# A hybrid SSD and dilated-attention block on one Trainium2 core: the value projection with weights stationary and tokens moving

## The chip, the core and the metric

The kernel runs on one core of a Trainium2 chip. A core has a matrix engine (TensorE, in the profile PE for matmuls and PEld for loads of the stationary operand), three engines for elementwise work (VectorE or DVE, ScalarE or ACT, GpSimd or POOL) and a queue that issues DMAs (SyncE or SP). The engines run side by side and meet at semaphores; each takes its instructions in order. TensorE writes to PSUM, and VectorE and ScalarE bring results from there to SBUF.

The metric is the device time in microseconds of one execution of the whole block. The profile is of one such execution.

## The reference, cut to what matters

One layer, 1024 tokens, width 1024, all in float32. A normalised input `h` is multiplied by one wide matrix `w_in`, whose columns are split over a state-space branch (SSD), an attention branch and two gates:

```python
h = rmsnorm(x, norm_mix[l])
proj = h @ w_in[l]
z, xBC, dt_raw, qkv, gate_logits = jnp.split(proj, offs[1:], axis=-1)
...
qkv = qkv.astype(jnp.float32).reshape(b, S, 3, ATT_N_HEADS, ATT_HEAD_DIM)
q = rope(qkv[:, :, 0], pos)
k = rope(qkv[:, :, 1], pos)
v = qkv[:, :, 2]
y_att = dilated_attention_branch(q, k, v).reshape(b, S, ATT_OUT_DIM).astype(x.dtype) @ w_att_out[l]
```

There are 12 heads of 128 features in three groups of four. The groups differ in their dilation: a head of the second group lets token t see tokens t, t-4, t-8 and so on, so its tokens are sorted into residue classes, and attention runs in blocks of 128 tokens of one class. After attention the three groups are mixed per token, then come the gates, an output projection, and a SwiGLU feed-forward.

## The kernel before

**Dense units.** All projections are cut into units that TensorE works through one after the other. Each float32 operand is split into a rounded part (hi) and a remainder (lo), and each product takes three matmuls (`mm3`, L336): hi with hi, hi with lo, lo with hi. The normalised input lies in SBUF as `hhi` and `hlo`, with features on the partitions and the 1024 tokens in natural order along the free dimension. A unit writes into one of two wide PSUM pieces (`wide`, 1024 float32 columns, two banks); `wide_now` (L325) takes one, and the task that brings the result out frees it.

There are two kinds of units. `unit_a` (L462) makes 128 output features for all 1024 tokens: the weights are the stationary operand, 512 tokens move, 2 x 8 x 3 = 48 matmuls; the result has features on the partitions. `unit_b` (L474) makes 256 output features for 512 tokens: 128 tokens of `hhi` or `hlo` are stationary, 256 columns of weights move, 2 x 4 x 4 x 3 = 96 matmuls; the result has tokens on the partitions. Which tokens are stationary is said by a function `sel`. For the value projection it is `sel_dil` (L1073): with stride r, the 128 tokens of block b are r elements apart in `hhi`:

```python
res.append(t[:, k, :].rearrange("p (l r) -> p r l", r=4)[:, b // 2, (b % 2) * P:(b % 2 + 1) * P])
```

`STRIDE = (1, 4, 8)` (L41) gives r for the three groups. So the values leave PSUM as rows of tokens in block order, which is how the product of probabilities and values wants them.

**Weights.** `plan` (L344) makes a list of loads in the order of use; `w_dma` fetches the next one over SP (512 KB each), and `w_split` (L354) makes hi on ScalarE (a cast) and lo on VectorE. `pump` keeps at most three loads ahead.

**Order.** The instruction streams are written by a planner, `Pace` (L174). It holds an own time for TensorE and the other engines from a table of costs (`cost`, L188; it knows nothing of strides). Everything but the dense units is a generator: it yields the tiles it waits for, and is continued when the planner believes that they are due. It is looked at only in `tick` (L383), which a unit calls after every second k-tile, that is after six matmuls in `unit_a` and after twelve in `unit_b`. So background work enters TensorE's queue at these places, and if a tile is late against the plan, TensorE waits with all that stands behind.

**Attention.** Two halves (`sp`), three groups each, two heads per half and group. For such a pair the units were: key and query of the first head, two `unit_b` for the values of both heads (L1125), key and query of the second head. `rope_task` (L837) rotates keys and queries and writes them sorted by residue class; it needs three free slabs for a key and two for a query (`slabs`, SBUF pieces of 1024 columns, L312). `v_task` (L867) copies values out of PSUM on ScalarE, 512 columns at a time. `head_bg` (L880) does the attention of one head in the background: scores, exponentials, transposes of the probabilities into one of four PSUM banks (`bank`, L315), product with the values. The heads run one after the other (`att_bg`, L1050); `stats_out` and `combine` (L994) mix the groups and store the result in DRAM (`att_d`). Behind the attention units follow 16 gate units, the first 12 of which run while the last of this is still under way (L1284). The last group of the state-space branch runs beside the first pair.

Of the kernel before, what the change touches and what calls it, by code (L numbers as in the profile page):

```python
# [18 lines left out]
DRAM = bass.MemoryType.DRAM  # L19

P = 128
S = 1024
# [15 lines left out]
QKV0 = DT0 + NH  # L38
GATE0 = QKV0 + 3 * 12 * P

STRIDE = (1, 4, 8)  # L41
# [31 lines left out]


class Buf:
    """A tile in a slot that goes back to its owner on free()."""

    def __init__(self, owner, slot, shape, dt):
        n = math.prod(shape[1:])
# [10 lines left out]
    def free(self):  # L90
        self.owner.pieces.append(self.slot)
        self.slot = None


class Slot:
    """A place in a pool; every use of it is a tile of its own type."""

    def __init__(self, pool, name, width):
        self.pool, self.name, self.width, self.n = pool, name, width, 0
# [4 lines left out]


class Store:
    """Slots of equal size, handed out in the order in which they came back."""

    def __init__(self, pieces, pace=None):
        self.pieces = deque(pieces)  # L110
# [34 lines left out]


class Engine:
    """Passes calls on to an engine and notes when their results are due."""

    def __init__(self, real, pace, kind):  # L150
        self.real, self.pace, self.kind = real, pace, kind
# [20 lines left out]


class Pace:  # L174
    """Emission order: dense tensor work in small pieces, and other tasks as soon as their inputs are due."""

    def __init__(self):
        self.t = 0.0
# [117 lines left out]
def hybrid_block(ctx, tc, x, norm_mix, w_in, b_gate, conv_w, conv_b, dt_bias, a_log, d_skip, ssm_norm,  # L296
                 w_ssm_out, w_att_out, w_mix_out, norm_ffn, w_ffn_gate, w_ffn_up, w_ffn_down, norm_final,
                 consts, rope, out):
    pace = Pace()
    nc = Core(tc.nc, pace)  # L300
    x, out = x[0], out[0]
    w_in, w_ssm_out, w_att_out, w_mix_out = w_in[0], w_ssm_out[0], w_att_out[0], w_mix_out[0]
# [9 lines left out]
    slabs = Store([Slot(cpool, f"slab{i}", 1024) for i in range(N_SLAB - 6)])  # L312
    halves = Store([Slot(hfp, f"half{i}", 512) for i in range(12)])
    wide = Store([Slot(pp, f"wide{i}", 1024) for i in range(2)])
    bank = Store([Slot(pp, f"bank{i}", 512) for i in range(4)], pace)  # L315
# [9 lines left out]
    def wide_now():  # L325
        while not wide.pieces:
            pace.idle()
        return wide.get([P, 1024])
# [4 lines left out]
    def tp(o, i, ident):  # L333
        nc.tensor.transpose(o, i, ident)
# [3 lines left out]
        mm(o, lh, rl, False, False)  # L338
        mm(o, ll, rh, False, last)

    # ---------------------------------------------------------------- weight stream
    loads, wstate = [], {"dma": 0, "split": 0, "use": 0}

    def plan(src, nk):  # L344
        loads.append({"src": src, "shape": [P, nk, src.shape[-1]]})
        return len(loads) - 1
# [24 lines left out]
    def w_get(i):  # L371
        while wstate["split"] <= i:
            while wstate["dma"] <= i:
                w_dma()
            w_split()
        wstate["use"] = i
        return loads[i]["w"]
# [5 lines left out]
    def tick():  # L383
        pump()
        pace.due()

    def cols_of(w, k0, nk, c0, nc_):
        return w[k0 * P:(k0 + nk) * P, c0:c0 + nc_].rearrange("(k p) c -> p k c", p=P)
# [20 lines left out]
    def small(tag, w):  # L409
        return cpool.tile([P, w], F32, tag=f"{tag}{w}", name=f"{tag}{w}_{nid()}", bufs=4)  # L410

    # ---------------------------------------------------------------- scratch in DRAM
    acs_d = dr.tile([NCH * NH, P], F32, name="acs_d")
    ea_d = dr.tile([NCH * NH, P], F32, name="ea_d")
    yt_d = [[dr.tile([P, 4, 256], F32, name=f"yt_d{g}_{q}") for q in range(4)] for g in range(NG)]
# [2 lines left out]
    att_d = [dr.tile([P, S], F32, name=f"att_d{i}") for i in range(4)]  # L418
    x2_d = dr.tile([S, D], F32, name="x2_d")

    # ---------------------------------------------------------------- constants and small parameters
    ident = cpool.tile([P, P], F32, name="ident")
    nc.sync.dma_start(ident, consts[:, C_ID:C_ID + P])
    par = cpool.tile([P, 152], F32, name="par")
# [8 lines left out]
    dcol = cpool.tile([P, 16], F32, name="dcol")  # L433
    ysum = cpool.tile([P, NG, NCH], F32, name="ysum")

    # ---------------------------------------------------------------- generic dense units
    hhi = hp.tile([P, KD, S], F32R, tag="hhi", name="hhi")
    hlo = hp.tile([P, KD, S], F32R, tag="hlo", name="hlo")

# [3 lines left out]
    def plan_b(w, col):  # L443
        return [plan(cols_of(w, kh * 4, 4, col, 256), 4) for kh in range(2)]

    class Pair:
        """Two banks in place of a wide piece."""

        def __init__(self):
            while len(bank.pieces) < 2:  # L450
# [23 lines left out]
    def unit_b(lids, sel, last):  # L474
        ps = wide_now()
        for kh in range(2):
            hi, lo = w_get(lids[kh])
            for j in range(4):
                sl = slice(j * 256, j * 256 + 256)
                for kk in range(4):  # L480
                    k = kh * 4 + kk
                    lh, ll = sel(k, j)
                    mm3(ps.v[:, sl], lh, ll, hi[:, kk, :], lo[:, kk, :], k == 0 and j % 2 == 0, k == KD - 1 and j % 2 == 1)
                tick()
            if last:
                w_done(lids[kh])
        return ps

    # ================================================================ state-space branch
    eslabs = Store([slabs.pieces.popleft() for _ in range(2)])  # L490
    grp = [dict() for _ in range(NG)]
    seen = set()
# [56 lines left out]
        grp[g]["CT"] = u  # L549

    class Quarters:
        """Four slabs of a group, each with a quarter of the tokens of its four feature tiles."""

        def __init__(self, g, name, f):
            self.g, self.name, self.f = g, name, f
# [272 lines left out]
        ea.free()  # L828
        pace.fire("dt")

    # ================================================================ attention branch
    rp = {}
    maskA = cst[:, C_MA - P:C_MA - P + 512]
    maskB = cst[:, C_MB - P:C_MB]
    att = {}
# [28 lines left out]
            rp[1].free()  # L864
        pace.fire(f"qk{which}_{head}")

    def v_task(h0, th, ps):  # L867
        if th == 0:
            yield from slabs.room(2)
            for i in range(2):  # L870
                att["v", h0 + i] = slabs.get([P, 8, P])
        v = ps.v.rearrange("p (j c) -> p j c", j=4)
        yield [ps]
        for i in range(2):
            nc.scalar.copy(att["v", h0 + i].v[:, th * 4:(th + 1) * 4, :], v[:, :, i * P:(i + 1) * P])
        ps.free()
        if th == 1:
            pace.fire(f"v{h0}")

    def head_bg(sp, gi, i):  # L880
        head = gi * 4 + sp * 2 + i
        yield f"qk0_{head}"
        yield f"qk1_{head}"
        yield f"v{gi * 4 + sp * 2}"
        yield [att[0, head], att[1, head], att["v", head]]
        q, k, v = att[0, head].v, att[1, head].v, att["v", head].v
        r = STRIDE[gi]
# [7 lines left out]
        for b0 in range(0, 8, step):  # L895
            yield from bank.room()
            yield from halves.room()
            ps, scb = bank.get([P, 512]), halves.get([P, 512])
            sc = scb.v
            segs = []  # L900
            for bi in range(step):
                b = b0 + bi
# [11 lines left out]
            four = lambda a: a.rearrange("p (a b) -> p a b", a=4)  # L914
# [20 lines left out]
            pt, pT = bank.get([P, 512]), halves.get([P, 512])  # L935
# [130 lines left out]
        t.free()  # L1066
        pace.fire(f"gate{i}")

    # ================================================================ dense programme of the input projection
    def sel_nat(th):  # L1070
        return lambda k, j: (hhi[:, k, (th * 4 + j) * P:(th * 4 + j + 1) * P], hlo[:, k, (th * 4 + j) * P:(th * 4 + j + 1) * P])

    def sel_dil(r, th):  # L1073
        def sel(k, j):
            b = th * 4 + j
            res = []
            for t in (hhi, hlo):
                if r == 1:
                    res.append(t[:, k, b * P:(b + 1) * P])
                elif r == 4:  # L1080
                    res.append(t[:, k, :].rearrange("p (l r) -> p r l", r=4)[:, b // 2, (b % 2) * P:(b % 2 + 1) * P])
                else:
                    res.append(t[:, k, :].rearrange("p (l r) -> p r l", r=8)[:, b, :])
            return res
        return sel

    units = []

    def add_a(col, task):
        lids = plan_a(col)  # L1090

        def run(ps=None):
            ps = unit_a(lids, ps)
            pace.spawn(task(ps), 0.0, -1)
        units.append(run)

    def add_b(col, sels, tasks):
        lids = plan_b(w_in, col)
        for th in range(2):
            def run(th=th):  # L1100
                ps = unit_b(lids, sels[th], th == 1)
                pace.spawn(tasks[th](ps), 0.0, -1)
            units.append(run)

    def add_z(g):
        for f in range(4):
# [10 lines left out]
    first = [plan_a(XBC0 + DI)[0], plan_a(XBC0 + DI + 512)[0]]  # L1117
# [4 lines left out]
    def add_qk(which, gi, head):  # L1122
        add_a(QKV0 + (which * 12 + head) * P, lambda ps: rope_task(which, head, STRIDE[gi], ps))

    for sp in range(2):  # L1125
        for gi in range(3):
            h0 = gi * 4 + sp * 2
            add_qk(1, gi, h0)
            add_qk(0, gi, h0)
            add_b(QKV0 + (24 + h0) * P, [sel_dil(STRIDE[gi], 0), sel_dil(STRIDE[gi], 1)],  # L1130
                  [lambda ps, th=th, h0=h0: v_task(h0, th, ps) for th in range(2)])
            add_qk(1, gi, h0 + 1)
            add_qk(0, gi, h0 + 1)
    n_before_gates = len(units)
    for i in range(16):
        add_a(GATE0 + i * P, lambda ps, i=i: gate_task(i, ps))

    # ================================================================ normalised input, transposed; first units on its quarters
    xts = [slabs.get([P, D]) for i in range(NCH)]
    nm, ptmp = slabs.get([P, D]), slabs.get([P, 2, P])  # L1140
    jks = [slabs.get([P, D]) for i in range(2)]
# [153 lines left out]
    halves = Store([Slot(hfp, f"last{i}", 512) for i in range(2)])  # L1295
    slabs.pieces.extend(eslabs.pieces)

    # ================================================================ gated merge, output projection, second norm
    mplans = []
    for th in range(2):  # L1300
        for o in range(KD):
# [158 lines left out]
    for th in range(2):  # L1460
# [10 lines left out]
        for cb in range(4):  # L1471
            def sel(k, j):
                pace.until(f"mx{th}{k}")
                return (h2["hi"][:, 1, k, j * P:(j + 1) * P], h2["lo"][:, 1, k, j * P:(j + 1) * P])

            ps = unit_b(mplans[th * 12 + 8 + cb], sel, True)
            pace.spawn(mo_task(th, cb, ps), 0.3, -1)

    # ================================================================ feed-forward
    act = {}  # L1480

    def ffn_task(f, th, ps):
# [50 lines left out]
    order = [(th, k) for th in range(2) for k in range(KF)]  # L1533
# [56 lines left out]
    for th in range(2):  # L1590
        outs = {}
        tiles = (0, 1, 2, 3) if th else (2, 3, 0, 1)
# [73 lines left out]
```

## Time and profile before

| | |
|---|---|
| median of three runs | 2450.73 us (2450.6 to 2452.07) |
| the profiled execution, from its first to its last instruction | 2448.2 us |
| instructions | 29021 |
| attention's units, first key unit to first gate unit | about 587 to 1185 us |
| mean granted TensorE clock | 0.993 |
| DMA, mean over the span | 90 GB/s |

The page gives no time for the profiled execution other than its span; the median of the runs is 2.5 us above it.

How to read it: a row of the page or of a view names the engine, the operation, the tile written and the tiles read (`out<-in`, with the running number of each tile), the shapes as partitions x elements, and a count or times. Nearly all rows have the line L157, that of the helper that passes calls on to the engines, so tiles tell instructions apart: `wide__33_7663` is one use of a wide PSUM piece, so one unit. A matmul's duration runs from its start to its modelled end, and matmuls overlap; how fast they follow one another is seen in their starts.

### The profile page before, as it was taken

The page shows a single profiled execution, that of the slowest core. Times are in us where ns is not written, and L with a number is a line of the kernel's source. Part 1 is how long each engine was busy: PE and PEld are TensorE (multiplying, and loading weights), DVE is VectorE, ACT ScalarE, POOL GpSimd, SP SyncE. Part 2 cuts the span into 40 slices and gives each one's busy share as a digit, 9 for nine tenths or more (in the row PEclk, how much of TensorE's full clock was granted, in tenths as well). Part 3 has the DMA queues.
Part 4 walks back from the last instruction along what each step waited for, and adds up shares of the span by engine and source line. Part 5 has one row for each costly group of instructions (what it writes and reads, how often), then busy time and mean ns, then how long its engine had stood idle before and what let it go on. Part 6 is the DMA issues. An engine that isn't in the chain of part 4 may idle for free. (4 is left out here: it accounts for less than half of the span.)

```text
span 2448.2 us, 29021 instructions
## 1 busy us (share of the span) xinstructions
PE 2395.4 (98%) x11952; PEld 2021.1 (83%) x11952; DVE 1067.9 (44%) x1542; ACT 734.3 (30%) x1293; POOL 315.8 (13%) x196
## 2 busy tenths in 40 slices
PE   6999999999999999999999998999999999999998
PEld 6887878878889988989888887889888888888786
DVE  6557485765642334332442246534312222233544
ACT  3335253443532233231323224323211111123332
POOL 3005041241520112010040003000000000000101
PEclk8999999999999999999999999999999999999999
DMA  3124242332411013011274456454111111123242
GB/s 122 51 74 122 69 121 73 104 102 88 121 44 35 18 44 112 18 44 27 65 239 127 137 158 196 137 166 127 44 42 45 52 52 44 44 98 117 95 155 78
DMA packets 255016, 220.72 MB, mean 90 GB/s; under 512 B 17132, under 2 KB 226980, under 8 KB 254884
## 3 DMA queue, kind: packets, MB, share of 16 engines
q1 hardware_dynamic: 254884, 218.87, 29.4%
q8 instruction: 94, 1.54, 0.3%
q14 instruction: 38, 0.31, 0.0%
HBM read 191.18 MB, written 27.66 MB: 89 GB/s over the span
## 5 line engine op out<-in xcount | busy, mean ns | idle before, releaser
L157 POOL TENSOR_TENSOR xr<-xr,nfin 128x512 f32<-128x512 f32 x16 | 20.3, 1299 | 915.7 <-ACT jk L157 915.7
L157 POOL TENSOR_TENSOR slab__13_10497<-slab__13_10497,last__3_10482 128x1024 f32<-128x1024 f32 x1 | 2.4, 2409 | 178.9 <-DMA slab__13_10497<-yt_d 178.9
L157 POOL TENSOR_TENSOR half__1_1316<-slab__2_1111,dcol 128x512 f32<-128x512 f32 x1 | 1.0, 1044 | 130.0 <-DVE slab__2_1111 L157 130.0
L157 ACT ACTIVATE jk<-xr 128x512 f32<-128x512 f32 x16 | 10.0, 625 | 24.3 <-DVE xr L157 24.3
L157 PE MATMUL wide__50_10579<-slab__44_10622,h2hi 128*128 128x256 f32 x16 | 5.4, 337 | 6.8 <-DVE slab__44_10622 L157 6.8
L157 ACT ACTIVATE xr<-xr,or 128x512 f32<-128x512 f32 x8 | 5.8, 724 | 17.6 <-DVE or L157 17.6
L157 DVE TENSOR_TENSOR slab__21_6711<-slab__23_6648,slab__20_6710 128x1024 fp32r<-128x1024 f32 x1 | 1.2, 1226 | 21.9 <-ACT slab__20_6710 L157 21.9
L157 DVE TENSOR_TENSOR slab__30_8576<-slab__33_8513,slab__27_8575 128x1024 fp32r<-128x1024 f32 x1 | 1.2, 1225 | 21.9 <-ACT slab__27_8575 L157 21.9
L157 DVE SCALAR_TENSOR_TENSOR ot<-or,ov 128x1 f32<-128x1 f32 x24 | 10.2, 427 | 0.6
L157 POOL TENSOR_TENSOR slab__9_8030<-slab__9_8030,slab__6_4726 128x1024 f32<-128x1024 f32 x1 | 2.4, 2395 | 61.2 <-ACT slab__9_8030 L157 61.2
L157 POOL TENSOR_TENSOR slab__6_6165<-slab__6_6165,slab__6_4726 128x1024 f32<-128x1024 f32 x1 | 2.4, 2398 | 61.2 <-ACT slab__6_6165 L157 61.2
L157 POOL TENSOR_TENSOR slab__7_6789<-slab__7_6789,slab__6_4726 128x1024 f32<-128x1024 f32 x1 | 2.4, 2412 | 60.5 <-ACT slab__7_6789 L157 60.5
L157 POOL TENSOR_TENSOR slab__10_8654<-slab__10_8654,slab__6_4726 128x1024 f32<-128x1024 f32 x1 | 2.4, 2412 | 60.5 <-ACT slab__10_8654 L157 60.5
L157 PE MATMUL wide__1_156<-hhi,slab__1_223 128*128 128x256 f32 x32 | 10.1, 316 | 0.0
L157 PE MATMUL wide__1_156<-hlo,slab__1_223 128*128 128x256 f32 x32 | 9.8, 307 | 0.2 <-DVE hlo L157 0.2
L157 PEld LDWEIGHTS wide__50_10579<-slab__44_10622,h2hi 128*128 128x128 f32 x16 | 3.8, 238 | 7.0 <-DVE slab__44_10622 L157 7.0
L157 PE MATMUL wide__1_157<-hhi,slab__1_274 128*128 128x256 f32 x32 | 9.0, 282 | 0.6 <-DVE slab__1_274 L157 0.6
L157 PE MATMUL wide__1_156<-hhi,slab__1_224 128*128 128x256 f32 x32 | 9.6, 299 | 0.0
L157 DVE TENSOR_TENSOR rt<-rs 128x2 f32<-128x2 f32 (+2 forms) x30 | 9.0, 301 | 1.0
L157 PE MATMUL wide__1_157<-hhi,slab__1_273 128*128 128x256 f32 x32 | 9.3, 291 | 0.0
L157 PE MATMUL wide__1_157<-hlo,slab__1_273 128*128 128x256 f32 x32 | 9.0, 281 | 0.0
L157 PE MATMUL bank__1_158<-ident 128*128 128x128 f32 x36 | 6.3, 357 | 2.6 <-DMA ident<-in_consts 2.6
(6145 smaller groups left out, 8396.5 us busy)
## 6 DMA issues: line engine op xcount, KB each, us to landing
xr<-x_d SPq DMA_DIRECT2D x8, 512.0 KB, 7.3
out<-xr SPq DMA_DIRECT2D x16, 256.0 KB, 2.2
slab__1_123<-in_x SPq DMA_DIRECT2D x1, 512.0 KB
slab__1_124<-in_x SPq DMA_DIRECT2D x1, 512.0 KB
slab__1_131<-in_norm_mix SPq DMA_DIRECT2D x1, 512.0 KB
slab__1_138<-in_w_in SPq DMA_DIRECT2D x1, 512.0 KB, 7.9
slab__1_125<-in_x SPq DMA_DIRECT2D x1, 512.0 KB
slab__1_126<-in_x SPq DMA_DIRECT2D x1, 512.0 KB
```

The source lines that it names most:

```text
L157: r = call(*args, **kw)
```

## The change

The values become a `unit_a` for each head, like keys and queries: the weights of 128 features are stationary, 512 tokens in natural order move. The result has features on the partitions. `v_task` copies it out of PSUM on ScalarE and reads it sorted by residue class (r elements apart) while writing it in one piece into a slab `t`. Then eight transposes on TensorE, four to a PSUM bank, turn it into rows of tokens, and two copies on ScalarE bring these to the slab `V`. The order of the units of a head is key, query, value; a head waits for its own values instead of the pair's. Loads of the value weights have 8 k-tiles of 128 columns instead of 4 k-tiles of 256.

```diff
-    def v_task(h0, th, ps):
-        if th == 0:
-            yield from slabs.room(2)
-            for i in range(2):
-                att["v", h0 + i] = slabs.get([P, 8, P])
-        v = ps.v.rearrange("p (j c) -> p j c", j=4)
+    def v_task(head, r, ps):
+        yield from slabs.room(2)
+        t, V = slabs.get([P, S]), slabs.get([P, 8, P])
         yield [ps]
-        for i in range(2):
-            nc.scalar.copy(att["v", h0 + i].v[:, th * 4:(th + 1) * 4, :], v[:, :, i * P:(i + 1) * P])
+        nc.scalar.copy(t.v.rearrange("p (r l) -> p r l", r=r), ps.v.rearrange("p (l r) -> p r l", r=r))
         ps.free()
-        if th == 1:
-            pace.fire(f"v{h0}")
+        yield [t]
+        for q in range(2):
+            yield from bank.room()
+            pt = bank.get([P, 4, P])
+            for j in range(4):
+                b = q * 4 + j
+                tp(pt.v[:, j, :], t.v[:, b * P:(b + 1) * P], ident)
+            yield [pt]
+            nc.scalar.copy(V.v[:, q * 4:(q + 1) * 4, :], pt.v)
+            pt.free()
+        t.free()
+        att["v", head] = V
+        pace.fire(f"v{head}")
 
     def head_bg(sp, gi, i):
         head = gi * 4 + sp * 2 + i
         yield f"qk0_{head}"
         yield f"qk1_{head}"
-        yield f"v{gi * 4 + sp * 2}"
+        yield f"v{head}"
...
     for sp in range(2):
         for gi in range(3):
-            h0 = gi * 4 + sp * 2
-            add_qk(1, gi, h0)
-            add_qk(0, gi, h0)
-            add_b(QKV0 + (24 + h0) * P, [sel_dil(STRIDE[gi], 0), sel_dil(STRIDE[gi], 1)],
-                  [lambda ps, th=th, h0=h0: v_task(h0, th, ps) for th in range(2)])
-            add_qk(1, gi, h0 + 1)
-            add_qk(0, gi, h0 + 1)
+            for head in (gi * 4 + sp * 2, gi * 4 + sp * 2 + 1):
+                add_qk(1, gi, head)
+                add_qk(0, gi, head)
+                add_a(QKV0 + (24 + head) * P, lambda ps, head=head, gi=gi: v_task(head, STRIDE[gi], ps))
```

The functions `sel_nat`, `sel_dil` and `add_b` go; some comments and docstrings go too, which changes no instruction.

More of the change, by code (lines that the diff above doesn't have):

```diff
@@ L1067, in gate_task @@
         pace.fire(f"gate{i}")
[L1070 to L1085, printed above, removed]
     units = []
@@ L1095, in add_a @@
         units.append(run)
[L1097 to L1103, printed above, removed]
     def add_z(g):
```

## The prediction

> **What bounds the kernel now.** I read the page's busy times and its 40 slices first, to see which engine has no slack.
>
> ```profile
> PE 2395.4 (98%) x11952; PEld 2021.1 (83%) x11952; DVE 1067.9 (44%) x1542; ACT 734.3 (30%) x1293; POOL 315.8 (13%) x196
> ...
> PE   6999999999999999999999998999999999999998
> ...
> PEclk8999999999999999999999999999999999999999
> ```
>
> TensorE is busy in 98% of the span, ScalarE in 30%, VectorE in 44%, at a full granted clock after the first slice. "Busy" says that a matmul is in flight, not that it goes at its best rate. So the next view is the windows over the attention part of the input projection; its columns are the window, its length, busy time and count of instructions of PE, PEld, DVE, ACT and POOL, clock, DMA share and GB/s.
>
> ```profile
> 927.00:949.00 22.00, 22.00 (x196) 22.00 (x196) 7.30 (x21) 3.98 (x6) 7.17 (x3) 1.00 0.33 94
> 1005.00:1054.00 49.00, 49.00 (x228) 48.84 (x226) 10.30 (x11) 8.15 (x16) 2.38 (x1) 1.00 0.05 12
> 1054.00:1110.00 56.00, 55.84 (x279) 46.65 (x279) 25.91 (x31) 20.23 (x43) 7.19 (x3) 1.00 0.17 48
> 1110.00:1159.00 49.00, 49.00 (x217) 48.98 (x216) 7.92 (x11) 6.57 (x15) 2.39 (x1) 1.00 0.11 22
> ```
>
> The first row is the value projection of a stride-1 pair of heads, the second that of a stride-4 pair, the fourth that of a stride-8 pair; the third is four key and query units. The two strided V stages take 49 us for hardly more matmuls than the stride-1 stage does in 22. Their PEld column is full: weights are being loaded all the time, while DVE and ACT have next to nothing to do. This stage is bound by TensorE's weight loads, and no other engine waits behind it.
>
> To price one matmul I take the tile view, whose rows give duration (min/median/max) and the first and last start. Each row's 16 instructions stand at every third place, so 45 starts lie between the two times.
>
> ```profile
> L157 PEld LDWEIGHTS wide__31_7171<-slab__21_6893,hhi x16: 187/188/188, 938.1 to 943.2; 128*128 128x128 f32 x16
> L157 PE MATMUL wide__31_7171<-slab__21_6893,hhi x16: 276/276/276, 938.2 to 943.3; 128*128 128x256 f32 x16
> ...
> L157 PEld LDWEIGHTS wide__34_7802<-slab__27_7591,hhi x16: 332/332/333, 1043.2 to 1053.8; 128*128 128x128 f32 x16
> L157 PE MATMUL wide__34_7802<-slab__27_7591,hhi x16: 402/402/402, 1043.3 to 1053.9; 128*128 128x256 f32 x16
> ...
> L157 PEld LDWEIGHTS wide__37_8436<-slab__29_8223,hhi x16: 337/337/337, 1147.2 to 1158.0; 128*128 128x128 f32 x16
> L157 PE MATMUL wide__37_8436<-slab__29_8223,hhi x16: 403/403/403, 1147.4 to 1158.2; 128*128 128x256 f32 x16
> ...
> L157 PE MATMUL wide__40_8979<-hhi,slab__63_8825 x16: 388/388/388, 1223.9 to 1234.2; 128*128 128x512 f32 x16
> ```
>
> Start to start, a 256-column matmul takes 5.1/45 = 0.113 us at stride 1, 10.6/45 = 0.236 us at stride 4 and 10.8/45 = 0.240 us at stride 8. A 512-column one of a gate unit (the last row; key and query units run the same code) takes 10.3/45 = 0.229 us. Only the stationary operand differs between the first three: 128 token columns next to each other, or 4 or 8 elements apart. The strided weight load lasts 332 to 337 ns instead of 188 and can't hide behind 256 moving columns.
>
> **The change part by part.**
>
> *V matmuls.* Each of the six pairs has two units of 96 matmuls: 4 units, 384 matmuls, of each stride. Removed: 384 x 0.113 = 43.4, 384 x 0.236 = 90.6 and 384 x 0.240 = 92.2, together 226.2 us. Added: 12 units of 48 matmuls over 512 columns, weights stationary and tokens in natural order: 576 x 0.229 = 131.9 us. Difference **-94.3 us**, all on the path, since PE has no idle time in these windows.
>
> *Transposes.* 12 heads x 8, in 24 groups of four. The timeline of TensorE shows such a group of the attention background between matmuls of a unit:
>
> ```profile
> 1002.35 0.39 PE L157 MATMUL wide__33_7569<-hhi,slab__23_7435 128*128 128x512 f32 x1
> 1002.58 0.60 PE L157 MATMUL bank__68_7646<-ident,half__19_7621 128*128 128x128 f32 x4
> 1002.93 0.48 PE L157 MATMUL wide__33_7569<-hhi,slab__23_7434 128*128 128x512 f32 x1
> 1003.25 0.39 PE L157 MATMUL wide__33_7569<-hlo,slab__23_7434 128*128 128x512 f32 x1
> ```
>
> From the group's start to the second wide matmul behind it are 0.67 us; less one wide matmul (0.23) the group costs 0.44 us, its disturbance of the stream included. 24 x 0.44 = **+10.6 us**. The Trainium skill, page "TensorE: Matmul & The Clock Gate", section "Part 4: PE-mode transpose", speaks against the change here: it gives about 275 ns for one 128x128 transpose inside a kernel, and by that, as an estimate, the 96 would cost 26.4 us. The row above gives 0.11 us each, so the row decides; the page's price is kept below as a rival.
>
> *Waiting for the copy out of PSUM.* This is the new wait. The first four transposes of a head stand in PE's queue at the first tick behind the V unit's end, that is behind six matmuls of the next unit: 6 x 0.229 = 1.37 us. They wait for ScalarE's copy of all 1024 tokens. Behind them in PE's in-order queue stands the whole next unit, so a late copy stops TensorE. These rows bound it:
>
> ```profile
> L157 PE MATMUL wide__34_7802<-slab__23_7526,hhi x16: 396/402/485, 1030.6 to 1042.6; 128*128 128x256 f32 x16
> ...
> 1030.81 0.58 ACT L157 COPY slab__9_7815<-wide__33_7663 128x512 f32<-128x512 f32 x1 [2.96 <-PE wide__33_7663 L157]
> ...
> L157 ACT ACTIVATE slab__11_9055<-wide__40_8979,par x1: 1127/1127/1127, 1235.1 to 1235.1; 128x1024 f32<-128x1024 f32 x1
> ...
> 1037.77 0.69 DVE L157 COPY slab__10_7390<-bank__69_7765 128x512 f32<-128x512 f32 x1 [11.05 <-PE bank__69_7765 L157]
> ...
> 1135.91 1.08 DVE L157 COPY slab__11_8029<-bank__78_8378 128x512 f32<-128x512 f32 x1 [8.43 <-PE bank__78_8378 L157]
> ...
> 1170.95 1.19 DVE L157 COPY slab__9_8211<-bank__79_8626 128x512 f32<-128x512 f32 x1 [3.33 <-PE bank__79_8626 L157]
> ```
>
> ScalarE starts 0.2 us after a unit's end (the next unit begins at 1030.6, the copy at 1030.81). A contiguous pass over 1024 PSUM columns takes 1.13 us, so it ends 1.33 us behind the unit, just ahead of the transposes: no wait. Whether reading PSUM 4 or 8 elements apart is slower on ScalarE no row shows. The only strided copies are VectorE's, which write strided: 1.08 and 1.19 us against 0.69, a factor of 1.57 and 1.72. By these the copy takes 1.77 and 1.94 us, and PE would wait 0.60 and 0.77 us for each of the 4 heads of either stride: 4 x 0.60 + 4 x 0.77 = 5.5 us. Below, nothing excludes that it is as fast as the contiguous one: 0. Above, doubling both factors' excess (2.13 and 2.45 times the contiguous pass) gives 4 x 1.23 + 4 x 1.60 = 11.3 us. I take **+5.5 us**, from the rows nearest in having a stride. The Trainium skill, page "Advanced Engine Details and Errata", section "Memory Cachelines", says that consecutive PSUM elements should come in adjacent pairs for best throughput; it gives no time. By it the sum would keep these 5.5 us, and without it would drop them; no row of this run shows which.
>
> *ScalarE and the pieces.* Out go 24 copies of 512 columns, in come 12 of 1024 and 24 of 512: about 12 x 1.13 = 13.6 us more on ScalarE (1.8 times that if strided reads are slow), which has 70% idle. The wide PSUM piece goes back 1.3 to 2.2 us behind its unit and is wanted one unit, 11 us, later. If that cover went, each head would cost the excess of the copy over 11 us.
>
> *Loads.* Two loads of 512 KB per pair stay two; their rows in DRAM shrink from 1 KB to 512 B, which key and query loads have already, and these run at a DMA share of 0.17 without PE idling (third windows row, 55.84 of 56). SP issues them in the same queue, one per 11 us where there were two per 49. Cost: 0, covered by three loads ahead.
>
> *Background.* The second head's V unit moves behind its key and query units, and each head can start when its own V is ready. Heads run one after the other. In the third windows row a unit with background takes 56/4 = 14 us, so three units offer a head some 41 us. I see no new bound. The tail after the last head is the combine, whose last store is at 1254.4; the gate units that cover it run to 1322.8:
>
> ```profile
> L157 SPq DMA_DIRECT2D att_d<-slab__10_7390 x1: 320/320/320, 1254.4 to 1254.4; - x1
> ...
> 1185.40:1322.80 137.40, 136.69 (x618) 112.49 (x617) 57.14 (x60) 42.56 (x62) 32.99 (x13) 1.00 0.55 169
> ```
>
> So up to 68 us of delay of that tail relative to the gates are free. What follows the gates keeps its distances.
>
> **Sum.** 2448.2 - 94.3 + 10.6 + 5.5 = 2370.0 us for the span. The page gives no other time for this execution; the median of the three runs, 2450.73, is 2.5 us above it, which I leave as it is: **2372.5 us**, 3.2% less.
>
> **The rivals.**
>
> *The transposes wait longer* (0.11).
>
> ```profile
> L157 ACT COPY slab__9_8030<-wide__34_7925 64x1024 f32<-64x1024 f32 x2 | 2.0, 1010 | 2.2 <-PE wide__34_7925 L157 2.2
> ...
> L157 ACT CAST slab__24_7932<-slab__59_7886 128x1024 fp32r<-128x1024 f32 x1 | 1.0, 1048 | 10.7 <-DMA slab__59_7886<-in_w_in 10.7
> ```
>
> PE's queue is in order, and a copy that finds a weight cast (1.05 us) or the two copies of a rope unit (2.0 us) ahead of it comes that much later, at every head: 12 x 1 to 12 x 2 = 12 to 24 us more: 2385 to 2397. For it: the emission order rests on planned times. Against: the V copies of before started 0.2 us after their unit.
>
> *The price of a transpose is higher* (0.03). A group placed directly behind a unit could lose more of the stream than the one shown; at 0.275 us each they add 15.8 us: 2388. The page on TensorE named above has this figure; the rows contradict it.
>
> *The gain is not handed on* (0.03). Attention's chain, or the gate stage behind it, sets the end. With the attention part shortened but its background not, the combine would have to slip by more than 68 us; half of the gain lost, 42 us, gives 2415. Against: 41 us offered per head, and PE never idles there now.
>
> *Slower than before: slabs* (0.03). A V task now takes two slabs at once for each head while it holds its wide piece. If they come free only when a background head ends, the unit after next can't start. The saving is 94.3 - 10.6 = 83.7 us, or 7.0 us per head; one further unit (11 us) still runs, so the change loses from a wait of 18 us per head on. At a whole head's 41 us it is 12 x 30 = 360 us, near 2730. Against: a key rope takes three slabs at a time now, and PE has 0.16 us idle in 1054 to 1110. With head h0 starting before K1 and Q1 arrive, fewer tiles are alive, not more.
>
> *The change doesn't do what it says* (0.01). If 256 moving columns and not the stride made the slow rate, stride 1 would show it; it has 0.113.
>
> **How the numbers follow.** The forecast has 0.79; within it the copy may cost 0 to 11.3 us, 2367 to 2378.3, and the stage's other small waits some us either way (beside the first pair runs the last group of the state-space branch, where PE is idle for 1.9 of 102.8 us):
>
> ```profile
> 587.40:690.20 102.80, 100.90 (x681) 85.31 (x680) 67.68 (x107) 52.19 (x108) 46.68 (x33) 1.00 0.39 111
> ```
>
> That makes 2361 to 2384. Its reach with part of the first two rivals holds 8 in 10: 2361 to 2388. Faster by over 0.2% (5 us, about what a measurement here can tell): forecast, first, second and third rival, 0.96. Slower: the slab rival, 0.03. Within 0.2%: 0.01.
>
> **What would show it.** V units as 48 matmuls at 0.229 us for every stride, no PEld row of 330 ns in the attention part; 96 transposes in groups of 0.44 us; the strided copy's duration on ScalarE, near 1.1 (then about 2367) or 1.8 to 1.9 us; PE idle in front of the first group of a head. The forecast is wrong if PE waits more than 2 us at the transposes, or if wide pieces come back late.

## The result, and the profile after

The changed kernel takes 2365.89 us (median of four runs, 2364.59 to 2366.54) against 2451.16 us before (2450.6 to 2452.07): ratio 0.9653, 95% interval 0.964 to 0.9667. That is 85.3 us less; the prediction had said 78.2 us less (2372.5 us). The profiled execution has a span of 2364.8 us against 2448.2, 83.4 us less.

The page's busy times and slices after:

```profile
PE 2310.4 (98%) x11472; PEld 1911.0 (81%) x11472; DVE 1070.8 (45%) x1542; ACT 747.4 (32%) x1305; POOL 316.4 (13%) x196
...
PE   6999999999999999999999989999999999999997
...
PEclk8999999999999999999999989999999999999999
```

TensorE is still the bound at 98%. PE has 480 matmuls fewer: 1152 of 256 columns went, 576 of 512 columns and 96 transposes came. ScalarE has 13 us more work, as counted, and no matmul of the attention stage waits for it. To see where the time went, the windows view is taken over the same three stretches of both kernels: the attention units, the 16 gate units, and all that follows. Before:

```profile
587.40:1185.40 598.00, 595.08 (x3144) 534.62 (x3143) 243.57 (x313) 191.69 (x399) 104.09 (x57) 1.00 0.20 54
...
1185.40:1366.70 181.30, 180.59 (x809) 148.51 (x808) 62.05 (x64) 50.76 (x70) 32.99 (x13) 1.00 0.50 156
1366.70:2448.20 1081.50, 1054.20 (x5009) 876.15 (x5007) 394.37 (x572) 259.33 (x393) 40.70 (x24) 0.99 0.31 98
```

After:

```profile
588.00:1099.80 511.80, 509.94 (x2656) 424.12 (x2655) 250.22 (x315) 203.82 (x410) 107.29 (x58) 1.00 0.24 63
...
1099.80:1281.00 181.20, 181.20 (x817) 149.37 (x816) 57.69 (x62) 51.17 (x71) 30.78 (x12) 1.00 0.51 156
1281.00:2364.80 1083.80, 1054.59 (x5009) 876.38 (x5007) 395.20 (x572) 259.97 (x393) 40.38 (x24) 0.99 0.31 98
```

The attention stage lost 86.2 us (598.0 to 511.8). The gates are the same to 0.1 us. The rest took 2.3 us longer in this execution with the same count of instructions; in the eight profiles of the runs below the same stretch is 1081.1 to 1083.0 us long, so most of that is scatter between executions. The stretch ahead of the attention stage is 0.6 us longer, also at the same instructions. The gain arose in one stage and was handed on whole.

The tile view of a stride-1, a stride-4 and a stride-8 value unit shows what became of the weight loads:

```profile
L157 PEld LDWEIGHTS wide__30_6842<-hhi,slab__21_6660 x16: 187/188/188, 884.2 to 894.5; 128*128 128x128 f32 x16
L157 PE MATMUL wide__30_6842<-hhi,slab__21_6660 x16: 387/388/389, 884.5 to 894.8; 128*128 128x512 f32 x16
...
L157 PEld LDWEIGHTS wide__35_7672<-hhi,slab__24_7508 x16: 187/188/193, 1007.2 to 1019.8; 128*128 128x128 f32 x16
L157 PE MATMUL wide__35_7672<-hhi,slab__24_7508 x16: 392/394/585, 1007.3 to 1020.0; 128*128 128x512 f32 x16
...
L157 PEld LDWEIGHTS wide__38_8224<-hhi,slab__26_8059 x16: 187/188/188, 1088.6 to 1098.9; 128*128 128x128 f32 x16
L157 PE MATMUL wide__38_8224<-hhi,slab__26_8059 x16: 388/388/389, 1088.8 to 1099.1; 128*128 128x512 f32 x16
```

No load of 330 ns is left: these take 188 ns, and none in the stage takes more than 193. The first and the last unit have no background between their matmuls, and over 45 steps from start to start 10.3 us pass: 0.229 us per matmul, at stride 1 as at stride 8.

The new wait would be seen in these views: the copies' rows on ScalarE, the timelines of ScalarE (one row) and TensorE around the transposes of a stride-4 head, the tile view of the slab that this copy writes, and the waits of TensorE's matmuls in this stage.

```profile
L157 ACT COPY slab__11_6922<-wide__30_6842 128x1024 f32<-128x1024 f32 x1 | 1.0, 1015 | 7.9 <-PE wide__30_6842 L157 7.9
...
L157 ACT COPY slab__13_7767<-wide__35_7672 128x1024 f32<-128x1024 f32 x1 | 1.0, 1014 | 3.0 <-PE wide__35_7672 L157 3.0
...
L157 ACT COPY slab__11_8295<-wide__38_8224 128x1024 f32<-128x1024 f32 x1 | 1.0, 1014 | 7.9 <-PE wide__38_8224 L157 7.9
```

```profile
1020.90 1.01 ACT L157 COPY slab__13_7767<-wide__35_7672 128x1024 f32<-128x1024 f32 x1 [2.96 <-PE wide__35_7672 L157]
...
1021.85 0.40 PE L157 MATMUL wide__35_7758<-hhi,slab__25_7606 128*128 128x512 f32 x1
1022.08 0.60 PE L157 MATMUL bank__76_7770<-ident,slab__13_7767 128*128 128x128 f32 x4
1022.44 0.48 PE L157 MATMUL wide__35_7758<-hhi,slab__24_7605 128*128 128x512 f32 x1
1022.76 0.39 PE L157 MATMUL wide__35_7758<-hlo,slab__24_7605 128*128 128x512 f32 x1
```

```profile
L157 PE MATMUL bank__76_7770<-ident,slab__13_7767 x4: 273/273/273, 1022.1 to 1022.4; 128*128 128x128 f32 x4
...
who waited for it (us, times):
...
  PEld bank__76_7770 L157: 0.2, 1
```

```profile
PE bank__55_5386 L157 <- DVE slab__16_5289 L157: 0.8, 1, 0.8
PE bank__48_5125 L157 <- POOL slab__7_5089 L157: 0.7, 1, 0.7
PE bank__46_4944 L157 <- POOL slab__6_4893 L157: 0.3, 1, 0.3
```

The copy takes 1.01 us at stride 1, 4 and 8 alike (the first three rows, in this order). At stride 4 it ends at 1021.91, and the transposes start at 1022.08, 0.23 us behind the matmul before them, so without a gap. Only the load of their stationary operand, which runs beside the matmuls, stands 0.2 us for the copy (last row of the slab's tile view). The three waits in the last view make up 1.8 of the 1.9 us that TensorE is idle in the stage, and none of them is for a value copy. From the group's start to the second wide matmul behind it are 0.68 us; less one wide matmul (0.23) the group costs 0.45.

### The profile page after: what moved, and what is told of

It is laid out like the page before. It is cut to its first block, busy times and chain, and to the rows that moved or that the text cites. A ratio compares the mean times of both kernels' runs of the same rounds, so it can differ in the third digit from the quotient of the medians.

```text
span 2364.8 us, 28089 instructions
## 1 busy us (share of the span) xinstructions
PE 2310.4 (98%) x11472; PEld 1911.0 (81%) x11472; DVE 1070.8 (45%) x1542; ACT 747.4 (32%) x1305; POOL 316.4 (13%) x196
## 5 line engine op out<-in xcount | busy, mean ns | idle before, releaser
L157 POOL TENSOR_TENSOR slab__13_10065<-slab__13_10065,last__3_10050 128x1024 f32<-128x1024 f32 x1 | 2.4, 2400 | 180.7 <-DMA slab__13_10065<-yt_d 180.7
L157 PE MATMUL wide__50_10147<-slab__43_10190,h2hi 128*128 128x256 f32 x16 | 6.0, 373 | 6.9 <-DVE slab__43_10190 L157 6.9
L157 DVE SCALAR_TENSOR_TENSOR slab__15_8816<-slab__11_8763,par,slab__12_8815 128x512 fp32r<-128x512 f32 x2 | 4.9, 2489 | 9.4 <-ACT slab__12_8815 L157 9.4
L157 PEld LDWEIGHTS bank__1_158<-ident 128*128 128x128 f32 x36 | 6.1, 193 | 2.7 <-DMA ident<-in_consts 2.7
L157 PE MATMUL wide__50_10147<-slab__43_10148,h2hi 128*128 128x256 f32 x16 | 5.2, 324 | 2.9 <-ACT slab__43_10148 L157 2.9
```

Source lines behind the costliest of these rows:

```text
L157: r = call(*args, **kw)
```

## The experiments

The theory after this: the gain is the strided weight load (-94.3), the transposes cost 0.11 us each on the path (+10.6), and the copy costs nothing. Each part was tested by itself. Each ratio is to the kernel before on the same chip. It took 2450.26 us beside the changed kernel run again, the doubled transposes, the stride-1 pairs and the strided write; 2450.89 beside the stride alone, the copy in order and the strided moving operand; 2450.7 beside the strided load behind 512 columns. The changed kernel was run again on the first of these chips only, so what is held against it from the second compares across chips.

### The changed kernel again

> The changed kernel as it is, on the same chip as the next three, to compare them with. About 2366 us; its span some 1 to 2 us less.

Measured: 2364.44 us (2363.11 to 2365.89), ratio 0.9652 (0.9639 to 0.9665).

### The stride alone

```diff
-            add_b(QKV0 + (24 + h0) * P, [sel_dil(STRIDE[gi], 0), sel_dil(STRIDE[gi], 1)],
+            add_b(QKV0 + (24 + h0) * P, [sel_dil(1, 0), sel_dil(1, 1)],
```

> The kernel before with one edit: the 128 stationary tokens of every value unit are neighbours (stride 1 for all groups), so values of the strided groups come out in the wrong order; the count and shape of matmuls, loads and copies stay. Theory: the stride of the stationary operand is the whole cost, 384 x (0.236 - 0.113) + 384 x (0.240 - 0.113) = 96 us less: 2355 us, below the changed kernel by its 10.6 us of transposes. Rival: the form with 256 moving columns, or the wait for weight loads as such, is the cost: about 2451 us.

Measured: 2356.33 us (2356.06 to 2356.65), ratio 0.9614 (0.9599 to 0.9628): 94.6 us less than before, 96 expected, and 8.1 us below the changed kernel on the other chip, where 10.6 were expected. The tile view of a stride-8 unit of this kernel:

```profile
L157 PEld LDWEIGHTS wide__28_6571<-slab__20_6358,hhi x16: 187/188/188, 819.0 to 824.1; 128*128 128x128 f32 x16
L157 PE MATMUL wide__28_6571<-slab__20_6358,hhi x16: 276/276/276, 819.1 to 824.2; 128*128 128x256 f32 x16
```

Same shape, same count, same code; only the step between the stationary tokens changed, and this unit runs at the stride-1 rate (5.1/45 = 0.113 us). The rival, that 256 moving columns are slow as such, falls.

### The strided load behind 512 columns

```diff
+    def unit_wide(lids, sel, last):
...
+            for j in range(2):
+                sl = slice(j * 512, j * 512 + 512)
...
+                    lh, ll = sel(k, j)
+                    c = kk // 2 * 2
+                    mm3(ps.v[:, sl], lh, ll, hi[:, c:c + 2, :], lo[:, c:c + 2, :], k == 0, k == KD - 1)
...
-                  [lambda ps, th=th, h0=h0: v_task(h0, th, ps) for th in range(2)])
+                  [lambda ps, th=th, h0=h0: v_task(h0, th, ps) for th in range(2)], unit_wide if gi else unit_b)
```

> The kernel before, with the value units of the stride-4 and stride-8 pairs at 48 matmuls instead of 96: the same strided tokens are stationary, but 512 weight columns move (two k-tiles side by side) and only two of the four token blocks of a unit are computed, so the values of these groups are not those of the reference. It asks how the strided weight load and the moving columns add up. Theory A, they run side by side and the longer one counts: 0.236 us per matmul as with 256 columns, 8 x 48 x 0.236 = 91 us instead of 183, about 2359 us. Theory B, the excess of the strided load (0.236 - 0.113 = 0.123 us) comes on top of the stream: 0.229 + 0.123 = 0.352 us, 135 us instead of 183, about 2403 us.

Measured: 2361.8 us (2359.3 to 2363.18), ratio 0.9636 (0.962 to 0.9652): theory A (2359), not B (2403). The weight load of a stride-4 unit in the tile view, and the first and the last of 21 matmuls of this unit in TensorE's timeline, which has no other work between them:

```profile
L157 PEld LDWEIGHTS wide__34_7558<-slab__23_7334,hhi x8: 308/310/313, 974.8 to 979.8; 128*128 128x128 f32 x8
```

```profile
975.70 0.40 PE L157 MATMUL wide__34_7558<-slab__23_7334,hhi 128*128 128x512 f32 x1
...
980.47 0.39 PE L157 MATMUL wide__34_7558<-slab__23_7334,hlo 128*128 128x512 f32 x1
```

The load is nearly as long as it was (310 ns), but the matmuls follow at 4.77/20 = 0.239 us, with 512 columns as with 256 (0.236). So the strided load runs beside the stream, and what counted before was the longer of the two. The loads also overlap one another: one lasts 310 ns, yet one is done every 0.239 us. So the load's row betrays the stride, but its length is not the price of a matmul.

### The transposes, doubled and taken away

```diff
-                tp(pt.v[:, j, :], t.v[:, b * P:(b + 1) * P], ident)
+                for _ in range(2):
+                    tp(pt.v[:, j, :], t.v[:, b * P:(b + 1) * P], ident)
```

> The changed kernel with each of the 96 transposes issued twice into the same place. Theory: 0.11 us each, 96 x 0.11 = 10.6 us more: 2376.5 us. Rival 1, they are hidden: 2366. Rival 2, 0.275 us each: 26.4 us more, 2392.

Measured: 2375.0 us (2372.35 to 2376.57), ratio 0.9691 (0.9678 to 0.9705): 10.6 us above the changed kernel's 2364.44. Hidden transposes (0) and 0.275 us each (26.4) both fall.

```diff
-                add_a(QKV0 + (24 + head) * P, lambda ps, head=head, gi=gi: v_task(head, STRIDE[gi], ps))
+                if gi:
+                    add_a(QKV0 + (24 + head) * P, lambda ps, head=head, gi=gi: v_task(head, STRIDE[gi], ps))
+                elif head % 2 == 0:
+                    add_b(QKV0 + (24 + head) * P, [sel_nat(0), sel_nat(1)],
+                          [lambda ps, th=th, head=head: v_pair(head, th, ps) for th in range(2)])
```

`v_pair` is the `v_task` of before; it tells both heads of the pair that their values are there.

> The changed kernel, but the four stride-1 heads keep the old form (128 contiguous tokens stationary, 256 weight columns moving, two units per pair, no transposes). Theory: the form costs the same at stride 1 (0.113 us for 256 columns against 0.229 for 512), so only the 8 groups of transposes go, 8 x 0.44 = 3.5 us: about 2362.4 us. Rival 1, the transposes lie beside other work and cost nothing: 2366. Rival 2, a transpose costs 0.275 us: 8.8 us less, 2357.

Measured: 2360.4 us (2360.21 to 2361.1), ratio 0.9636 (0.9622 to 0.9649): 4.0 us below the changed kernel run beside it, 3.5 expected. In the windows view its attention stage is 3.4 us shorter than the changed kernel's 511.8:

```profile
587.50:1095.90 508.40, 506.74 (x2816) 429.49 (x2815) 248.28 (x315) 199.93 (x406) 106.69 (x58) 1.00 0.24 64
```

This version beats both kernels. The difference to the changed one is small (0.17%), but their runs don't overlap (2360.21 to 2361.1 against 2363.11 to 2365.89): where the stationary tokens are neighbours, the old form is as fast, and needs no transposes.

### The copy out of PSUM

Two runs ask whether the copy costs anything, and what would happen if it did. In the first it leaves the tokens in natural order.

```diff
-        nc.scalar.copy(t.v.rearrange("p (r l) -> p r l", r=r), ps.v.rearrange("p (l r) -> p r l", r=r))
+        nc.scalar.copy(t.v, ps.v)
```

> The changed kernel with the copy out of PSUM left in natural token order (values of the strided groups come out in the wrong order). Theory: the strided read costs ScalarE nothing and TensorE doesn't wait for it: 2366 us, no difference. Rival, the prediction's term: 5.5 us less than the changed kernel, 2360 us.

Measured: 2363.47 us (2363.15 to 2365.8), ratio 0.9645 (0.9629 to 0.9661), within the changed kernel's scatter (2363.11 to 2365.89, on the other chip). The twelve copies take 1012 to 1018 ns here, and 1012 to 1015 in the changed kernel: the strided read costs nothing. In the second the stride sits on the write:

```diff
-        nc.scalar.copy(t.v.rearrange("p (r l) -> p r l", r=r), ps.v.rearrange("p (l r) -> p r l", r=r))
+        nc.scalar.copy(t.v.rearrange("p (r l) -> p l r", r=r), ps.v.rearrange("p (l r) -> p l r", r=r))
```

> The changed kernel, with the reorder on the other side of the copy: PSUM is read in one piece and SBUF is written 4 or 8 elements apart by token. The copy that reads strided took 1.01 us, no more than a contiguous pass. Theory: a strided write is what VectorE's rows priced (factors 1.57 and 1.72), so this copy takes 1.6 and 1.7 us, ends 0.4 to 0.6 us behind the transposes' place in the queue, and TensorE waits there: some 4 us more in all, 2370 us. Rival: ScalarE writes strided as fast as it reads: 1.01 us, 2366 us.

Measured: 2370.45 us (2369.55 to 2370.8), ratio 0.9676 (0.9662 to 0.9689): 6.0 us above the changed kernel, 4 expected. ScalarE's rows by form and TensorE's waits of this kernel:

```profile
L157 ACT COPY slab__13_7767<-wide__35_7672 128x1024 f32<-128x1024 f32 x1 | 2.0, 1959 | 2.9 <-PE wide__35_7672 L157 2.9
L157 ACT COPY slab__11_8042<-wide__36_7943 128x1024 f32<-128x1024 f32 x1 | 2.0, 1958 | 2.9 <-PE wide__36_7943 L157 2.9
...
L157 ACT COPY slab__11_8295<-wide__38_8224 128x1024 f32<-128x1024 f32 x1 | 1.9, 1942 | 7.9 <-PE wide__38_8224 L157 7.9
L157 ACT COPY slab__11_6922<-wide__30_6842 128x1024 f32<-128x1024 f32 x1 | 1.0, 1017 | 7.9 <-PE wide__30_6842 L157 7.9
```

```profile
PE bank__76_7770 L157 <- ACT slab__13_7767 L157: 0.7, 1, 0.7
...
PE bank__81_8298 L157 <- ACT slab__11_8295 L157: 0.7, 1, 0.7
...
PE bank__60_5845 L157 <- ACT slab__8_5842 L157: 0.6, 1, 0.6
```

The copy takes 1.96 us at stride 4 (first row) and 1.96 or 1.94 at stride 8 (second and third row), against 1.02 at stride 1 (last row); 1.6 and 1.7 were expected. TensorE stands still for 0.6 to 0.7 us at each of the eight strided heads, together some 5.2 us. So the wait that the prediction feared is real, and about as long as it said (0.60 and 0.77 us). It begins where the copy isn't done some 1.2 us after its start (1020.90 to 1022.08 in the timelines above).

### The reorder inside the matmul

```diff
+        mv = lambda t, k, th: t[:, k, :].rearrange("p (l r) -> p r l", r=r)[:, th * r // 2:(th + 1) * r // 2, :] if r > 1 else t[:, k, th * 512:(th + 1) * 512]
...
-                mm3(ps.cut(sl.start, sl.stop), hi[:, k, :], lo[:, k, :], hhi[:, k, sl], hlo[:, k, sl], k == 0, k == KD - 1)
+                mm3(ps.cut(sl.start, sl.stop), hi[:, k, :], lo[:, k, :], mv(hhi, k, th), mv(hlo, k, th), k == 0, k == KD - 1)
...
-        nc.scalar.copy(t.v.rearrange("p (r l) -> p r l", r=r), ps.v.rearrange("p (l r) -> p r l", r=r))
+        nc.scalar.copy(t.v, ps.v)
```

> The changed kernel with the reorder moved into the matmul: weights stationary, the 512 moving tokens read from the normalised input 4 or 8 elements apart, and a contiguous copy out of PSUM. Theory A, a strided read costs TensorE the same per column on the moving side as on the weight side (144 ns for 128 columns, from 188 to 332): 0.58 us more for each of 384 matmuls, 221 us more, 2587 us. Theory B, only the weight load minds the stride: 2366 us.

Measured: 2446.45 us (2444.28 to 2450.55), ratio 0.9985 (0.9976 to 0.9994). Neither theory: 83.0 us above the run with the copy in order (2363.47, the same chip and the same plain copy), not 221 and not 0. A stride-4 and a stride-8 unit:

```profile
1069.46 0.66 PE L157 MATMUL wide__35_7672<-hhi,slab__24_7508 128*128 128x512 f32 x1
...
1075.90 0.66 PE L157 MATMUL wide__35_7672<-hhi,slab__24_7509 128*128 128x512 f32 x1
```

```profile
L157 PE MATMUL wide__38_8224<-hhi,slab__26_8059 x16: 592/610/612, 1160.7 to 1180.1; 128*128 128x512 f32 x16
```

Between the first two rows (TensorE's timeline, stride 4) lie 14 steps: 6.44/14 = 0.46 us per matmul. The stride-8 unit (tile view) has no background in it: 19.4/45 = 0.431 us. Both were 0.229. With these, 4 x 48 x 0.231 + 4 x 48 x 0.202 = 83.1 us: what was measured. A strided moving operand comes in at about half rate, 0.45 ns more per column at stride 4; taking the whole of the load's longer row (144 ns for 128 columns) as the price of a column was wrong.

## Why the prediction was right

**What bounds the kernel**: right. The undone stride alone gave 94.6 of the 96 us expected.

**V matmuls, -94.3**: right, by each part's own price: the new units run at 0.229 us for every stride.

**Transposes, +10.6**: right. Doubled they cost 10.6 us; a third of them taken away gave 4.0 for 3.5. The Trainium skill, page "TensorE: Matmul & The Clock Gate", section "Part 4: PE-mode transpose", gives about 275 ns for one transpose, timed on bf16, in one kernel. The trace agrees with this as the duration of one: each float32 transpose of the group at 1022.1 takes 273 ns. But they start 0.1 us apart and overlap, and the price in the stream is 0.11 us each. So the Trainium skill's figure and the rows agree, though the prediction says that they contradict each other; its rival took a duration for a price.

**Waiting for the copy, +5.5**: this term was mis-sized; it measured 0, as no matmul waits for a value copy. The mechanism is right, as the strided write shows. What failed is the choice of the row: VectorE's copies with 1.57 and 1.72 times the time write SBUF with a stride, and this copy reads PSUM with one. The forecast's own lower end, a copy as fast as the contiguous pass, was the answer; that pass, an activation, takes 1.13 us, and the copy 1.01. The sentence of the Trainium skill, page "Advanced Engine Details and Errata", section "Memory Cachelines", that consecutive PSUM elements should come in pairs for best throughput, does not show in this copy: 1014 ns at stride 4 and 8, 1015 at stride 1.

**Sum.** Without the mis-sized term it is 2448.2 - 94.3 + 10.6 = 2364.5 us; the span is 2364.8. That closeness is partly luck; it hides two small things: the attention stage lost 2.5 us more than the 83.7 foreseen, and the other stretches gave 2.8 back (0.6 ahead of it, 2.3 behind the gates, less 0.1 in the gates). Of the 2.5, TensorE's idle time in the stage, 2.92 us before and 1.86 after by the windows rows, is 1.1; the cause of the rest stays open. The windows view of the kernel with the stride alone undone says where it lies:

```profile
587.30:1090.10 502.80, 501.30 (x3144) 440.94 (x3143) 244.19 (x313) 191.90 (x399) 104.08 (x57) 1.00 0.23 64
```

Its attention stage is 95.2 us shorter than before, where 96 were foreseen. The changed form then adds 9.0 us (511.8), where the prediction's own prices give 131.9 - 1152 x 0.113 + 10.6 = 12.3 us. So the rest lies in the exchange of the form, not in the stride.

**ScalarE, loads, background, slabs**: right that they cost nothing. No wide piece came back late, and TensorE never stands for want of a free slab: the three waits shown above are for results of VectorE and GpSimd. The last store of the attention output is issued at 1162.0, 62 us behind the first gate unit's start (69 before):

```profile
L157 SPq DMA_DIRECT2D att_d<-slab__11_7030 x1: 383/383/383, 1162.0 to 1162.0; - x1
```

**The rivals.** Longer waits at the transposes, dearer transposes, a gain not handed on, the slab wait and a wrong cause did not come true; the last was tested by undoing the stride, the second by doubling the transposes, the others are read from the waits and the windows.

## What to carry to other kernels

Look at how a matmul's operands lie before looking at its shape: the same 96 matmuls took 11 or 23 us according to the step between the stationary columns, and the page's busy share of 98% told nothing of it; the duration of the weight load's row did, and the starts of the matmuls gave the price. In this kernel the cheap place for the reorder was where an engine with idle time reads PSUM, not the matmul and not the write to SBUF, and it was worth paying only for the tiles that need it. When a price is borrowed from another row, ask which side, which memory and which engine that row's stride is on.

## What was not expected of the hardware

- ScalarE reads float32 from PSUM 4 or 8 elements apart at no cost (1014 ns for 1024 columns), but takes 1942 to 1963 ns if it writes SBUF at these strides, 1.9 times as long.
- A strided stationary load is hardly felt behind a long stream: at stride 4 it costs 0.010 us behind 512 columns (0.239 against 0.229), but it doubles the time of a matmul with 256 (0.236 against 0.113).
- A strided moving operand halves the rate: 0.46 us at stride 4 and 0.431 at stride 8 for 512 columns, against 0.229. Stride 8 is the faster of the two here, and the slower of the two as a stationary operand (0.240 against 0.236).
